# Issuing Silu and its product after the next pair's first eviction, and moving the norms' inverse roots to GpSimd, in the MLP of a hybrid decoder block

## The chip, the cores and the metric

One Trainium2 chip, 8 cores, one program on each core. A core takes one half of one of four sequences (4096 of 8192 positions, plus a halo). The metric is the device time of the slowest core in microseconds. Most executions agree within 0.3%. Some fall in a slower state, in which the cores of one die show a lower granted TensorE clock. They are marked slow in each list of runs and are not compared here. The engines are PE (matmul), PEld (its weight loads), DVE (VectorE), ACT (ScalarE), POOL (GpSimd) and SP (SyncE, which issues transfers).

## The reference, cut to what matters

The block has a convolution branch and an attention branch, an output projection, then a gated MLP with a causal depthwise convolution of width 3 between up projection and activation, then a last RMSNorm. The change touches only the MLP and the norms around it:

```python
h = rms_norm(x, norm_ffn_g[layer])
up = causal_dwconv(h @ w_up[layer], ffn_conv_w[layer], ffn_conv_b[layer])   # 1024 -> 2 x 2816
gate, val = jnp.split(up, 2, axis=-1)
x = x + (jax.nn.silu(gate) * val) @ w_down[layer]                            # 2816 -> 1024
...
return rms_norm(x, final_norm_g)
```

## The kernel before

The kernel runs in three stages: projections and attention; convolution branch, gates and output projection; MLP. The third takes 48% of the span. It goes over nine tiles of positions (388, then 3 x 384, then 5 x 512 columns). Each tile has 22 pairs of up projections (one gate channel block, one value channel block) and then the down projection. One pair, cut to the order of issue:

```python
def c_pair(j, p):
    for q in range(2):                       # 0: gate half, 1: value half
        b = next_ps()                        # one of 8 PSUM banks
        fm(ps[b], wU[wi], ...)               # PE: 8 matmuls
        t = next_tmp()                       # one of 5 temporaries
        ACT: uc[...] = last two columns of ps[b]              # for the next tile's corner
        ACT: tmpC[t] = w2 * ps[b] + bias                      # the eviction
        for sh, wv_ in ((1, w1_), (2, w0_)):
            DVE: tmpC[t] += wv_ * ps[b] shifted by sh         # the two taps
        POOL: tmpC[t][:, 0:2] += corr[:, ch, :]               # corner correction
        if q == 0:
            ACT: actT[:, p] = Silu(tmpC[t])
        else:
            POOL: actT[:, p] = actT[:, p] * tmpC[t]           # the product
```

In the traces ScalarE, VectorE and GpSimd run their instructions in the order in which the kernel issues them: in the pair that the prediction shows, the eviction of the value half (2333.27 us) starts only after Silu (2332.68 us), which had waited 2.93 us. The norm of a block is a Square with accumulation on ACT, an inverse root of six tiny operations on DVE (`rsq`), and a multiply on DVE. Blocks of the next tile are normed after pairs 12 and 16 and within the down projection. At the end of each output block of the down projection, Square, inverse root, multiply and the store follow at once, in one of 4 residual buffers:

```python
S.add("act", ... Square, accum_out=ssq[:, col:col + 1])
rsq(128, col)                                # six tiny operations on DVE
S.add("dve", ... xr[sl] = xr[sl] * rstd * g3b)
S.add("sp", ... dma_start(out=out_d[...], in_=xr[sl]))
xr_load()
```

The softmax here doesn't subtract the row's maximum and nothing guards it: scores larger than these inputs give would overflow.

Of the kernel before, what the change touches and what calls it, by code (L numbers as in the profile page):

```python
# [14 lines left out]
D = 1024  # L15
# [113 lines left out]
def build_program():  # L129
# [177 lines left out]

    RC = 0.703952253

    def rsq(n, col):  # L310
        v, y, t = ssq[0:n, col:col + 1], rstd[0:n, col:col + 1], rtmp[0:n, col:col + 1]
        vk, yk, tk = ("ssq", col), ("rstd", col), ("rtmp", col)
        S.add("dve", lambda e: e.tensor_scalar(out=v, in0=v, scalar1=D * EPS, scalar2=None, op0=ALU.add),
              reads=[vk], writes=[vk])
        S.add("dve", lambda e: e.tensor_scalar(out=y.bitcast(I32), in0=v.bitcast(I32), scalar1=-0.5,
                                               scalar2=float(0x5F1FFFF9), op0=ALU.mult, op1=ALU.add),
              reads=[vk], writes=[yk])
        for lim in (2.38924456, 3.0 / RC ** 2):
            S.add("dve", lambda e: e.tensor_scalar(out=t, in0=v, scalar1=y, scalar2=y, op0=ALU.mult, op1=ALU.mult),  # L319
                  reads=[vk, yk], writes=[tk])  # L320
            S.add("dve", lambda e: e.tensor_scalar(out=y, in0=t, scalar1=lim, scalar2=y, op0=ALU.subtract, op1=ALU.mult),  # L321
                  reads=[tk, yk], writes=[yk])

    def scale_g(gap, key):
# [70 lines left out]

    stat_i = [0]

    def norm_front(xap, xkey, hbap, hbkey, n, gb, gkey):
        col = stat_i[0] % 16
        stat_i[0] += 1  # L400
        S.add("act", lambda e: e.activation(out=hbap[0:n, :], in_=xap[0:n, :], func=AF.Square,  # L401
                                            accum_out=ssq[0:n, col:col + 1]),
              reads=[xkey], writes=[hbkey, ("ssq", col)])
        rsq(n, col)
        S.add("dve", lambda e: e.scalar_tensor_tensor(  # L405
            out=hbap[0:n, :], in0=xap[0:n, :], scalar=rstd[0:n, col:col + 1], in1=gb[0:n, :],
            op0=ALU.mult, op1=ALU.mult), reads=[xkey, ("rstd", col), gkey], writes=[hbkey])
        note("act", 1240)
        note("dve", 1450)

    def norm_back(hbap, hbkey, n, dst, dkeys):
        t = next_ps()
# [842 lines left out]
    hbC = [buf("hbC%d" % i, W + 39424 + i * 2048, [128, D], BF16) for i in range(2)]  # L1255
    g2b = buf("g2b", W + 43520, [128, D], F32)
    xn = [buf("xn%d" % i, W + 47616 + i * 4096, [128, D], F32) for i in range(2)]
    xr = [buf("xr%d" % i, W + 55808 + i * 4096, [128, D], F32) for i in range(4)]
    g3b = buf("g3b", W + 72192, [128, D], F32)
    tmpC.append(buf("tmpC4", W + 76288, [128, 512], F32))  # L1260
    sem_g2, sem_g3 = newsem("s_g2"), newsem("s_g3")
    sem_xn = [newsem("s_xn%d" % i) for i in range(2)]
    sem_xr = [newsem("s_xr%d" % i) for i in range(4)]
    sem_out = [newsem("s_out%d" % i) for i in range(4)]
    S.add("sp", lambda e: e.dma_start(out=g2b, in_=g2_d.partition_broadcast(128)), writes=[("g2b",)], dma_sem=sem_g2)
    scale_g(g2b, ("g2b",))
    tmp_set["n"] = 5
    xn_list = [(0, -1)] + [(j, b) for j in range(9) for b in BB[j]]
    xn_l, cf, cb = [0], [0], [0]

# [8 lines left out]
        S.add("sp", lambda e: e.dma_start(out=xn[sl][0:n, :], in_=x1_d[r0:r0 + n, :]), reads=[("x1_d", blk)],  # L1279
              writes=[("xn%d" % sl,)], dma_sem=sem_xn[sl])  # L1280

    def c_front():
        i = cf[0]
        cf[0] += 1
        j, blk = xn_list[i]
        n = 4 if blk < 0 else 128
        norm_front(xn[i % 2], ("xn%d" % (i % 2),), hbC[i % 2], ("hbC%d" % (i % 2),), n, g2b, ("g2b",))
        xn_load()

    def c_back():  # L1290
# [10 lines left out]
    def xr_load():  # L1301
        i = xr_l[0]
        if i >= len(xr_list):
            return
        xr_l[0] += 1
        j, blk = xr_list[i]
        sl = i % 4
        S.add("sp", lambda e: e.dma_start(out=xr[sl], in_=x1_d[4 + 128 * blk:132 + 128 * blk, :]),
              reads=[("x1_d", blk)], writes=[("xr%d" % sl, 0), ("xr%d" % sl, 1)], dma_sem=sem_xr[sl])

    fw = fcw.rearrange("p (c k) -> p c k", k=3)

    def c_pair(j, p):
        w_ = BW[j]
# [5 lines left out]
        for q in range(2):  # L1320
# [10 lines left out]
            S.add("act", lambda e, b=b, t=t, ch=ch, w2_=w2_: e.activation(  # L1331
                out=tmpC[t][:, 0:n], in_=ps[b][:, o:w_], func=AF.Identity, scale=w2_, bias=fcb[:, ch:ch + 1]),
                reads=[("ps", b), "fcw", "fcb"], writes=[tk])
            for sh, wv_ in ((1, w1_), (2, w0_)):
                lo = max(0, sh - o)
                S.add("dve", lambda e, b=b, t=t, sh=sh, wv_=wv_, lo=lo: e.scalar_tensor_tensor(  # L1336
                    out=tmpC[t][:, lo:n], in0=ps[b][:, o + lo - sh:w_ - sh], scalar=wv_, in1=tmpC[t][:, lo:n],
                    op0=ALU.mult, op1=ALU.add), reads=[("ps", b), tk, "fcw"], writes=[tk])
# [2 lines left out]
                                                                    in1=corr[:, ch, :], op=ALU.add),  # L1341
                      reads=["corr", tk], writes=[tk])
            res.append(t)
            if q == 0:
                S.add("act", lambda e, t=t: e.activation(out=actT[:, p, 0:n], in_=tmpC[t][:, 0:n], func=AF.Silu),  # L1345
                      reads=[tk], writes=[("actT", p)])
            else:
                S.add("pool", lambda e, t=t: e.tensor_tensor(out=actT[:, p, 0:n], in0=actT[:, p, 0:n],  # L1348
                                                             in1=tmpC[t][:, 0:n], op=ALU.mult),
                      reads=[tk, ("actT", p)], writes=[("actT", p)])  # L1350

    def c_corr(j):
        par = j % 2
# [18 lines left out]
    def c_down(j, hooks):  # L1372
        ub_ = 0
        for bi, blk in enumerate(BB[j]):
            i = xr_i[0]
            xr_i[0] += 1
            sl = i % 4
            banks = [next_ps(), next_ps()]
            parts = ([(0, 0, 20), (1, 0, 20), (0, 20, 22), (1, 20, 22)] if bi == 0 else [(0, 0, 22), (1, 0, 22)])
            for hf, ka, kb in parts:  # L1380
                for k_ in range(ka, kb):
                    wt, wk_, kk = wdn(k_)
                    S.add("pe", lambda e, b=banks[hf], k_=k_, kk=kk, wt=wt, hf=hf: e.matmul(  # L1383
                        ps[b], lhsT=actT[:, k_, bi * 128:(bi + 1) * 128], rhs=wt[:, kk, hf * 512:(hf + 1) * 512],
                        start=(k_ == 0), stop=(k_ == 21), skip_group_check=True),
                        reads=[wk_, ("actT", k_)], writes=[("ps", banks[hf])])
                if kb == 22:
                    xs_ = xr[sl][:, hf * 512:(hf + 1) * 512]
                    S.add("dve", lambda e, b=banks[hf], xs_=xs_: e.tensor_tensor(out=xs_, in0=ps[b], in1=xs_, op=ALU.add),
                          reads=[("ps", banks[hf]), ("xr%d" % sl, hf)], writes=[("xr%d" % sl, hf)])  # L1390
                    if hooks:
                        hooks.pop(0)()
            col = stat_i[0] % 16
            stat_i[0] += 1
            t = next_tmp()
            S.add("act", lambda e, sl=sl, t=t, col=col: e.activation(
                out=tmpC[t].bitcast(BF16), in_=xr[sl], func=AF.Square, accum_out=ssq[:, col:col + 1]),
                reads=[("xr%d" % sl, 0), ("xr%d" % sl, 1)], writes=[("tmpC%d" % t,), ("ssq", col)])
            rsq(128, col)
            S.add("dve", lambda e, sl=sl, col=col: e.scalar_tensor_tensor(  # L1400
                out=xr[sl], in0=xr[sl], scalar=rstd[:, col:col + 1], in1=g3b, op0=ALU.mult, op1=ALU.mult),
                reads=[("xr%d" % sl, 0), ("xr%d" % sl, 1), ("rstd", col), ("g3b",)],
                writes=[("xr%d" % sl, 0), ("xr%d" % sl, 1)])
            S.add("sp", lambda e, sl=sl, blk=blk: e.dma_start(out=out_d[128 * blk:128 * (blk + 1), :], in_=xr[sl]),
                  reads=[("xr%d" % sl, 0), ("xr%d" % sl, 1)], dma_sem=sem_out[sl])
            xr_load()
        for h_ in hooks:
            h_()

    xn_load()  # L1410
    xn_load()
    for _ in range(1 + len(BB[0])):
        c_front()
        c_back()
    S.add("sp", lambda e: e.dma_start(out=g3b, in_=g3_d.partition_broadcast(128)), writes=[("g3b",)], dma_sem=sem_g3)
    scale_g(g3b, ("g3b",))
    for _ in range(4):
        xr_load()
    for j in range(9):
        if j > 0:  # L1420
            c_corr(j)
        for p in range(22):
            c_pair(j, p)
            if j + 1 < 9 and p in (12, 16):
                c_front()
        hooks = []
        if j + 1 < 9:
            n = len(BB[j + 1])

            def mk(m):  # L1430
                def f():
                    if m < n:
                        c_back()
                        if m + 2 < n:
                            c_front()
                return f
            hooks = [mk(0), mk(1), (lambda: None), mk(2), (lambda: None), mk(3)][:(6 if n == 4 else 4)]
        c_down(j, hooks)
        assert cb[0] >= 1 + sum(len(BB[q]) for q in range(min(j + 2, 9))), (j, cb[0])

    final_wait = [(s_, S.dma_count[s_]) for s_ in sem_out if S.dma_count.get(s_, 0)]
# [164 lines left out]
```

## Time and profile before

| | before |
|---|---|
| median of 5 first runs | 2723.28 us (2721.09 to 2733.06) |
| MLP stage, first up projection to last matmul, slowest core | 1419.2 to 2713.4 us |
| PE busy in the span | 77% |
| one pair at 512 columns | 5.02 us, of which PE's work is 16 matmuls |

The chain that ended last, asked for in the MLP stage alone, by line (share of that stretch):

```profile
by line: DVE arena L1336 21.2%; PE ps L1383 17.5%; issue 16.1%; PE ps L602 13.3%; POOL arena L1348 9.7%; ACT arena L1331 8.2%; POOL arena L1340 4.5%; ACT uc L1329 2.8%; PE ps L414 1.2%; DMA arena<-g 1.0%; DVE rtmp L319 0.8%; ACTq L1503 0.7%
```

L1336 are the taps, L1331 the evictions, L1340 the corrections, L1348 the products, L602 and L1383 the up and down matmuls. The other lines on which the case rests stand in the prediction. One is missing there: its cut of a pair leaves out the eviction of the value half, which starts as Silu ends and on which the first two taps of the group at 2334.14 us work. (The eviction that it shows, 2333.98 us, is already that of the next pair's gate half.)

```profile
2333.27 0.77 ACT L1331 ACTIVATE arena<-ps,fcb_s,fcw_s 128x512 f32<-128x512 f32 x1
```

### The profile page before, as it was taken

Reading aid. Unit: us, or ns where it says so; the run is one execution under the profiler, and the core shown is the slowest. Engines: PE = TensorE matmul, PEld = TensorE weight load, DVE = VectorE, ACT = ScalarE, POOL = GpSimd, SP = SyncE. Lnnn points to the kernel's source line nnn. Section 1 sums busy time; section 2 is a strip of 40 time slices with the busy share of each in tenths; the row PEclk is TensorE's granted clock in tenths of the full one; section 3 lists DMA queues with packets and bytes.
Section 4 is the critical chain, followed back from the end, with each engine's and each line's share of the span. In section 5 each row is a group of like instructions: output and inputs, shape, how many; then the busy total and the mean of one; then the engine's idle time right before and its main releaser. Section 6 shows DMA issues by size and latency. Waiting matters only on the chain.

```text
span 2721.7 us, 37992 instructions; the slowest of 8 cores (2705.1 to 2721.7 us)
## 1 busy us (share of the span) xinstructions
PE 2099.5 (77%) x11389; PEld 1050.1 (39%) x11550; DVE 1358.3 (50%) x2561; ACT 843.9 (31%) x1791; POOL 483.3 (18%) x826
## 2 busy tenths in 40 slices
PE   0677787854799999999946868686968778697877
PEld 0344444432455544444423434343424333242433
DVE  4554555511444444443325555555655565555554
ACT  1343344413222221112214343334332433323232
POOL 1000002304221111111211121222121212212131
PEclk9988898976899999999979999999999999899999
DMA  8443473496362223310595101010102010020100
GB/s 144 120 112 86 106 160 66 98 161 130 102 129 78 87 86 102 102 51 34 108 174 112 63 9 62 16 55 16 63 16 78 8 54 33 16 78 16 62 1 31
DMA packets 128319, 205.88 MB, mean 76 GB/s; under 512 B 9684, under 2 KB 90330, under 8 KB 127736
## 3 DMA queue, kind: packets, MB, share of 16 engines
q1 hardware_dynamic: 86072, 169.19, 21.3%
q0 software_dynamic: 42048, 34.26, 9.3%
q8 instruction: 98, 1.61, 0.3%
q14 instruction: 101, 0.83, 0.1%
HBM read 177.05 MB, written 60.63 MB: 87 GB/s over the span
## 4 chain that ended last, share of the span: by engine, by line
PE 47%; DVE 18%; issue 12%; POOL 8%; ACT 7%; DMA 7%; DVEq 1%; SPq 1%; ACTq 0%; POOLq 0%
PE ps L602 29%; DVE arena L1336 10%; PE ps L1383 8%; POOL arena L1348 5%; ACT arena L1331 4%; PE ps L1198 3%; PE ps L608 3%; DMA u_d<-arena 2%; POOL arena L1340 2%; DMA arena<-h_d 2%; PE ps L414 2%; ACT uc L1329 1%; DVE rtmp L319 1%; DVE rstd L321 1%; DVE arena L405 1%
## 5 line engine op out<-in xcount | busy, mean ns | idle before, releaser
L602 PE MATMUL ps<-arena 128*128 128x512 bf16 (+5 forms) x6749 | 1388.0, 362 | 232.9 <-DVE arena L1336 202.1
L602 PEld LDWEIGHTS ps<-arena 128*128 128x128 bf16 x6848 | 657.9, 99 | 929.4 <-issue 327.7
L1336 DVE SCALAR_TENSOR_TENSOR arena<-ps,fcw_s,arena 128x511 f32<-128x511 f32 (+4 forms) x792 | 530.4, 688 | 412.0 <-ACT uc L1329 263.1
L1383 PE MATMUL ps<-arena 128*128 128x512 bf16 x1372 | 329.1, 395 | 68.0 <-POOL arena L1340 33.7
L1345 ACT ACTIVATE arena<-arena 128x512 bf16<-128x512 f32 (+1 forms) x198 | 115.2, 582 | 583.5 <-POOL arena L1340 533.7
L1331 ACT ACTIVATE arena<-ps,fcb_s,fcw_s 128x512 f32<-128x512 f32 (+1 forms) x396 | 279.9, 731 | 0.0
L1383 PEld LDWEIGHTS ps<-arena 128*128 128x128 bf16 x1408 | 141.2, 101 | 243.9 <-issue 98.1
L1348 POOL TENSOR_TENSOR arena<-arena 128x512 bf16<-128x512 bf16 (+1 forms) x198 | 208.8, 1054 | 138.3 <-DVE arena L1336 95.8
L1340 POOL TENSOR_TENSOR arena<-arena,corr 128x2 f32<-128x2 f32 x352 | 69.3, 197 | 856.6 <-DVE arena L1336 812.7
L1166 DVE TENSOR_TENSOR arena<-ps,arena 128x512 f32<-128x512 f32 (+2 forms) x144 | 91.0, 633 | 251.7 <-PE ps L602 245.6
L1152 ACT ACTIVATE arena<-ps,bg_s 128x512 f32<-128x512 f32 (+2 forms) x144 | 92.1, 640 | 252.4 <-PE ps L602 252.4
L414 PE MATMUL ps<-ident,arena 128*128 128x128 bf16 (+2 forms) x656 | 62.1, 250 | 140.2 <-DVE arena L405 135.1
L252 ACT ACTIVATE arena<-ps 128x512 bf16<-128x512 f32 (+4 forms) x152 | 82.7, 544 | 214.0 <-PE ps L602 126.1
L608 PE MATMUL ps<-arena 128*128 128x256 bf16 (+2 forms) x676 | 122.1, 336 | 34.1 <-DMA arena<-h_d 32.9
L485 ACT ACTIVATE arena<-ps 128x512 bf16<-128x512 f32 x192 | 109.8, 595 | 118.2 <-PE ps L482 60.1
L506 PE MATMUL ps<-arena 128*128 128x66 bf16 x768 | 60.2, 206 | 92.7 <-DVE arena L489 46.0
L1169 POOL TENSOR_TENSOR arena<-arena 128x512 bf16<-128x512 f32 (+2 forms) x72 | 82.7, 1149 | 263.9 <-DVE arena L1166 237.9
L401 ACT ACTIVATE arena<-arena 128x1024 bf16<-128x1024 f32 (+1 forms) x82 | 86.3, 1053 | 137.1 <-PE ps L414 117.4
L489 POOL TENSOR_TENSOR arena<-arena,mask 128x512 bf16<-128x512 bf16 x64 | 72.1, 1153 | 278.0 <-ACT arena L485 277.7
L1198 PE MATMUL ps<-arena 128*128 128x512 bf16 (+1 forms) x514 | 116.8, 379 | 3.3 <-POOL arena L1169 2.5
L254 DVE CAST arena<-ps 64x512 bf16<-64x512 f32 (+1 forms) x95 | 65.4, 688 | 104.4 <-PE ps L602 81.2
L414 PEld LDWEIGHTS ps<-ident,arena 128*128 128x128 bf16 (+2 forms) x656 | 51.2, 114 | 164.1 <-issue 156.4
(86 smaller groups left out, 1255.7 us busy)
## 6 DMA issues: line engine op xcount, KB each, us to landing
arena<-x_loc SPq DMA_DIRECT2D x80, 512.0 KB, 4.4
arena<-x_d SPq DMA_DIRECT2D x64, 512.0 KB, 3.6
x_d<-arena SPq DMA_DIRECT2D x32, 512.0 KB, 4.2
out<-arena SPq DMA_DIRECT2D x32, 512.0 KB, 2.6
u_d<-arena SPq DMA_DIRECT2D x96, 132.0 KB, 3.1
arena<-u_d SPq DMA_DIRECT2D x32, 396.0 KB, 3.4
arena<-w_up POOLq DMA_DIRECT2D x22, 512.0 KB, 18.1
arena<-w_in POOLq DMA_DIRECT2D x10, 1024.0 KB, 27.9
```

Of the source, the lines that this page charges most:

```text
L414: S.add("pe", lambda e, kc=kc: e.transpose(out=psb[t][:, kc * 128:kc * 128 + n], in_=hbap[0:n, kc * 128:(kc + 1) * 128], identity=ident[0: ...
L485: S.add("act", lambda e: e.activation(out=PA[pi], in_=ps[sbk], func=AF.Exp, scale=0.125), reads=[("ps", sbk)], writes=[("PA%d" % pi,)])
L602: S.add("pe", lambda e, kc=kc: e.matmul(out, lhsT=wap[:, kc, col0:col0 + 128], rhs=rhs(kc), start=(kc == 0), stop=(kc == kcn - 1), skip_gr ...
L608: S.add("pe", lambda e, kc=kc: e.matmul(out, lhsT=lhs(kc), rhs=wap[:, kc, c0:c0 + n], start=(kc == 0), stop=(kc == KC - 1), skip_group_che ...
L1152: S.add("act", lambda e, b=b, t=t, br=br: e.activation(out=tmp[t][:, 0:w_], in_=ps[b][:, 0:w_], func=AF.Sigmoid, bias=bg[:, br * 8 + oc:br ...
L1198: S.add("pe", lambda e, b=b, kc=kc, hf=hf: e.matmul(ps[b][0:n, :], lhsT=mT[:, kc, c0:c0 + n], rhs=wO[:, kc, hf * 512:(hf + 1) * 512], star ...
L1331: S.add("act", lambda e, b=b, t=t, ch=ch, w2_=w2_: e.activation(out=tmpC[t][:, 0:n], in_=ps[b][:, o:w_], func=AF.Identity, scale=w2_, bias ...
L1336: S.add("dve", lambda e, b=b, t=t, sh=sh, wv_=wv_, lo=lo: e.scalar_tensor_tensor(out=tmpC[t][:, lo:n], in0=ps[b][:, o + lo - sh:w_ - sh], ...
L1340: S.add("pool", lambda e, t=t, ch=ch: e.tensor_tensor(out=tmpC[t][:, 0:2], in0=tmpC[t][:, 0:2], in1=corr[:, ch, :], op=ALU.add), reads=["c ...
L1345: S.add("act", lambda e, t=t: e.activation(out=actT[:, p, 0:n], in_=tmpC[t][:, 0:n], func=AF.Silu), reads=[tk], writes=[("actT", p)])
L1348: S.add("pool", lambda e, t=t: e.tensor_tensor(out=actT[:, p, 0:n], in0=actT[:, p, 0:n], in1=tmpC[t][:, 0:n], op=ALU.mult), reads=[tk, ("a ...
L1383: S.add("pe", lambda e, b=banks[hf], k_=k_, kk=kk, wt=wt, hf=hf: e.matmul(ps[b], lhsT=actT[:, k_, bi * 128:(bi + 1) * 128], rhs=wt[:, kk, ...
```

## The change

Its intent is to keep PE fed in the MLP stage, by not letting Silu stand in front of an eviction that DVE waits for, and by taking small work and waits off DVE. The core of the diff (cut):

```diff
-    tmpC.append(buf("tmpC4", ...))            # 5 temporaries, 4 residual buffers
+    tmpC += [... for i in range(3)]           # 7 temporaries, 3 residual buffers
@@ c_pair
             ACT eviction of half q
+            if q == 0:
+                flush(late)                   # Silu and product of the pair before
             DVE taps, POOL correction
-            if q == 0: ACT Silu
-            else:      POOL product
+        def gate(): ACT Silu; POOL product
+        late.append(gate)
+        if p == 0:
+            flush(finals)
@@ norms of the next tile's blocks
-            if p in (12, 16): c_front()       # Square, root on DVE, multiply
+            if p in (11, 15): c_stat()        # Square, root on POOL
+            if p in (13, 17): c_mul()         # multiply on DVE
@@ c_down, per output block
     DVE add to the residual
+    flush(finals)
     ...
-    rsq(128, col); multiply; store; xr_load() # root on DVE
+    norm_stat(..., "pool", ...)               # root on POOL
+    finals.append(fin)                        # multiply, store, load: behind the next add
```

Inside the down projection the norms of the next tile's third and fourth block are split into statistics and multiply in the same way. Nothing else changes.

## The prediction

> **What bounds the kernel now.** I read the page's slices first, then the waits from 1425 us on, then the order of time inside one pair, and last stretches of time side by side.
>
> ```profile
> PE 2099.5 (77%) x11389; PEld 1050.1 (39%) x11550; DVE 1358.3 (50%) x2561; ACT 843.9 (31%) x1791; POOL 483.3 (18%) x826
> PE   0677787854799999999946868686968778697877
> PEclk9988898976899999999979999999999999899999
> ```
>
> The changed lines run only in the last stage, the gated MLP: from 1419.2 us (first up projection) to the end, 48% of the span. Slices of 9 for PE in the stage before give way to a saw of 6 to 8. Each tooth is one of nine token tiles (388, 3 x 384, 5 x 512 columns): the low part is 22 pairs of up projections, the high part is the down projection.
>
> ```profile
> ACT arena L1345 <- POOL arena L1340: 533.7, 176, 5.4
> DVE arena L1336 <- ACT uc L1329: 263.1, 148, 2.9
> PE ps L602 <- DVE arena L1336: 202.1, 133, 3.1
> PE ps L1383 <- POOL arena L1340: 33.7, 10, 4.6
> PE ps L1383 <- POOL arena L1348: 31.9, 14, 3.7
> ```
>
> In the waits, every engine waits for another: Silu (L1345) for the corrected gate half, VectorE's taps for ScalarE, PE for VectorE to empty PSUM. None is full. Such a ring is a latency loop; one pair shows it.
>
> ```profile
> 2332.39 0.20 POOL L1340 TENSOR_TENSOR arena<-arena,corr 128x2 f32<-128x2 f32 x1
> 2332.68 0.63 ACT L1345 ACTIVATE arena<-arena 128x512 bf16<-128x512 f32 x1 [2.93 <-POOL arena L1340]
> ...
> 2333.98 0.79 ACT L1331 ACTIVATE arena<-ps,fcb_s,fcw_s 128x512 f32<-128x512 f32 x1
> 2334.14 3.11 DVE L1336 SCALAR_TENSOR_TENSOR arena<-ps,fcw_s,arena 128x511 f32<-128x511 f32 x4 [1.91 <-ACT uc L1329]
> 2335.89 0.20 POOL L1340 TENSOR_TENSOR arena<-arena,corr 128x2 f32<-128x2 f32 x1 [3.30 <-DVE arena L1336]
> 2336.29 1.16 POOL L1348 TENSOR_TENSOR arena<-arena 128x512 bf16<-128x512 bf16 x1 [0.20 <-POOL arena L1340]
> 2337.41 0.20 POOL L1340 TENSOR_TENSOR arena<-arena,corr 128x2 f32<-128x2 f32 x1
> ```
>
> The loop: the corner correction of a gate half (2332.39) releases Silu; in-order ScalarE evicts the value half only after Silu; VectorE needs two taps; GpSimd corrects, multiplies, and only then (2337.41) corrects the next pair's gate half. Period 5.02 us. In it VectorE works 3.11, GpSimd about 1.6, ScalarE 0.63 + 4 short and long evictions, about 2 us, and PE 16 matmuls. PE, eight banks ahead, is held to this pace.
>
> ```profile
> 2409.00:2523.00 114.00, 86.19 (x363) 35.72 (x369) 67.66 (x104) 45.76 (x108) 30.15 (x60) 0.95 0.07 22
> 2410.26 10.74 PE ps L602 x49
> ```
>
> The first row is 114 us of a 512-column up stage (columns: stretch, then PE, PEld, VectorE, ScalarE, GpSimd busy, clock): PE busy 86, but with bursts and half-speed spells. The second, from the chain, is a free run: 10.74 / 49 = 0.2192 us for a 512-column matmul, so a pair could cost 3.51 us.
>
> **What the Trainium skill says.** "TensorE: Matmul & The Clock Gate", section "What's actually happening", says the matmul clock falls to half after an idle window of about 3.4 us. The trace agrees: 0.95 or 0.96 in up stages with gaps, 1.00 where PE is dense. Its section "Seeing it yourself" warns that three cores of a die with dense matmuls are limited to 13/16. This trace disagrees:
>
> ```profile
> 800.00:1300.00 500.00, 482.84 (x2490) 240.15 (x2526) 213.22 (x372) 103.12 (x158) 69.03 (x81) 1.00 0.28 81
> ```
>
> This is the slowest core in the stage before, at 97% PE; all eight cores show 482 to 485 us busy and clock 1.00 there. "SBUF — State Buffer", section "Who interferes with whom", says a VectorE instruction with two SBUF inputs blocks against a GpSimd one that reads SBUF. The taps have one PSUM input, and they stay at 752 ns at most beside GpSimd's products: agrees. The norm multiply has two SBUF inputs, and its 1.28 us could meet a 1.16 us product, up to about a microsecond each time. "GPSIMD Engine Reference", section "2.1 Instruction dispatch", describes software dispatch for each instruction; here a 128x2 correction lasts 197 ns, and dependent GpSimd operations start 0.40 us apart.
>
> **The change part by part.**
>
> 1. Silu and product of a pair are issued late: after the next pair's gate eviction. ScalarE no longer meets a correction that has just begun to be computed, and GpSimd's product no longer stands between a tap and Silu. The shortest remaining ring is product, correction, Silu, each once per pair: 1.16 + 0.20 + 0.63 + about 0.4 of hand-overs = 2.4 us. The ring through value eviction and taps now spans two pairs: about 5.1 / 2 = 2.6 us. Both lie under 3.51, so at 512 columns PE sets the pace. Two more temporaries (seven, as one residual buffer goes) cover the later release.
>
> 2. The 6-step inverse root moves from VectorE to GpSimd: the four lines cost VectorE 33.3 + 26.1 + 9.4 + 9.1 = 78 us in the stage, mostly in down stages where VectorE is slack, but 2 x 2 us in each up stage. On GpSimd I estimate 6 x 0.42 = 2.5 us, twice in an up stage. It holds up the next correction: some 1.3 us of hole for VectorE each.
>
> 3. Norm statistics and multiply are split by two pairs, and the final multiply waits for the next addition. So VectorE no longer stands waiting 4 to 5 us at a tile's start, where it finishes the last block before pair 0 (2409.0 to 2414.2). One 1.28 us multiply goes behind pair 0.
>
> 4. Residual slots 4 to 3: a block takes 44 x 0.2192 = 9.65 us, a slot has two blocks, 19 us, for a store of 2.6 and a load of 3.6. Hidden.
>
> **Tile times.** Tile starts, read from PE's chain, are 1419.2, 1549.4, 1679.1, 1808.5, 1938.8, 2094.5, 2252.0, 2408.9, 2566.1, and the last matmul ends at 2713.4.
>
> 512 columns: up 352 x 0.2192 = 77.2; down 176 x 0.2192 = 38.6; four transposes of blocks at about 0.45 extra (2388.87 to 2389.31) = 1.8. Sum 117.6, taken as 118, four times, against 155.7 to 157.5. VectorE has 22 x 3.11 + 3 x 1.28 = 72.3, under 77.2. Down starts with 40 matmuls, 8.8 us, before it needs the last two pairs, which are ready about 4 us after the last up matmul. So its wait (65.6 us in all, the last two wait lines) goes too. Last tile, no transposes: 116 against 147.3.
>
> 384 columns: a free run is 17.06 us for 104 (164 ns), so 352 x 0.164 = 57.7, down 132 x 0.2192 = 28.9, transposes 1.4: 88.0. VectorE is level here: four taps in 2.58, a pair at about 2.61, PE's pair 2.62. With 3 x 1.28 of multiplies and 2 x 1.3 of holes VectorE needs 64 us, starts 2.2 us behind PE, and PE's down would need the last pairs at 66.5; I add a wait of about 1.5. Three tiles at 89.5, 89.5 and 91 (the last has a transpose right before the next tile), against 129.8, 129.4, 130.3.
>
> Tile 0: its first eviction stays at 1431.4, as ScalarE waits there for a DMA of g. Then VectorE, 22 x 2.61 + 5, to about 1495, and the rest of down 21 + 1.4: end near 1518, 98.5 us against 130.2. The down weights land by about 1465, before they are needed.
>
> Sum: 98.5 + 270 + 472 + 116 = 956.5 against 1294.2: 337.7 saved. The tail after the last matmul (8.3 us) grows by 0.6, as the inverse root takes 2.5 instead of 1.93 on it. 2723.3 - 337.7 + 0.6 = 2386. I add 4 us for hand-overs I don't see: 2390.
>
> **The rivals.** (a) The clock: if the denser last stage trips the 13/16 limit, its matmuls take 1.23 times as long: 950 x 0.23 = 218 us back, about 2610. Against it stands the 500 us stretch at 1.00 on all cores; for it, that VectorE and ScalarE are busier in this stage. (b) VectorE or GpSimd becomes the bound: if small GpSimd operations with a register operand last a microsecond, an inverse root blocks the corrections 6 us, twice a tile, and VectorE, level at 384, cannot catch up: 4 to 6 us a tile, about 2430. The 0.2 us rows speak against. (c) The wait only moves: products come later, so PE waits before down as now. That would give back up to 65.6 us, about 2455; but that wait came from VectorE lagging four pairs, which a PE-bound loop does not build up. (d) Nothing gained since PE is bound: excluded by 3.51 against 5.02.
>
> **Range and chances.** The sum is bounded by PE from below: no tile can beat it, except by my additions, so low is 2372. Above, (b) and part of (c) give 2430. Only (a) in full leaves that range, and even it is 4% faster. Predicted 2390, range 2372 to 2430; faster 0.97, same 0.02, slower 0.01.
>
> **What would show it.** PE's slices from 1430 us should read 9, the clock 1.00, a 512 tile 118 us, a 384 tile about 90, the span of a pair 3.5. ScalarE's wait for the correction and PE's for VectorE should nearly vanish, the latter staying in 384 tiles if anywhere. Inverse-root steps appear on GpSimd at 0.2 to 0.3 us. If pairs still take over 4 us, I missed a ring; if PE's matmuls are slower than 0.22 us in free runs, it is the clock.

## More of the kernel before

No line dominates: the chain walks around all four engines. That is what a latency ring looks like in this view.

## The result, and the profile after

| | before | after |
|---|---|---|
| median of all runs | 2727.38 us (16 runs, 5 of them slow) | 2370.15 us (9 runs, 2 of them slow) |
| profiled run | 2723.27 us | 2365.35 us |
| ratio of fast runs | | 0.8688, 95% interval 0.8674 to 0.8703 |
| MLP stage, slowest core | 1294.2 us | 938.1 us |

A ratio is the mean time of one kernel's fast runs over that of the other's in the same rounds, so it is not quite the ratio of the medians. The change is 13.1% faster; the two slow runs of the changed kernel took 2529.08 and 2700.80 us, the five of the kernel before 2773.41 to 2921.54. The prediction said 2390, with 2372 as its low end: the result lies 2 us below the range.

The page of the changed kernel: busy time, then PE's and the clock's slices. The MLP stage begins at the end of slice 24 of 40, the 3 among the nines.

```profile
PE 2040.4 (86%) x11550; PEld 1050.1 (44%) x11550; DVE 1275.0 (54%) x2195; ACT 856.2 (36%) x1791; POOL 613.8 (26%) x1192
PE   0578768794659999999999939999999999999998
PEclk9999889997759999999999969999999999999999
```

The saw is gone: PE reads 9 from the entry of the stage on, but for the last slice (8), which holds the tail. The chain of the MLP stage is now PE alone for long pieces (columns: start, length, what):

```profile
by line: PE ps L608 55.1%; PE ps L1409 29.8%; issue 3.2%; DVE arena L1358 3.0%; PE ps L420 1.4%; DMA arena<-g 1.3%; DVE arena L409 0.9%; DMA arena<-x_d 0.9%; POOL arena L1371 0.8%; ACT arena L1351 0.6%; POOL arena L1362 0.3%; POOL rtmp L319
...
1893.26 75.97 PE ps L608 x352
```

A whole up stage of 352 matmuls at 512 columns (L608) is one piece of 75.97 us with no wait in it. The waits of the stage, which answer to the list in the prediction (L1362 correction, L1369 Silu, L1358 taps, L1371 product):

```profile
ACT arena L1369 <- POOL arena L1362: 95.7, 82, 3.3
...
DVE arena L1358 <- ACT uc L1349: 30.6, 14, 13.3
...
PE ps L1409 <- POOL arena L1362: 2.8, 3, 0.9
...
PE ps L608 <- DVE arena L1358: 1.5, 1, 1.5
...
PE ps L1409 <- POOL arena L1371: 0.6, 1, 0.6
```

Silu's wait fell from 533.7 to 95.7 us, the taps' from 263.1 to 30.6, PE's for the taps from 202.1 to 1.5, and PE's before the down projection from 65.6 (33.7 + 31.9) to 3.4. What is left of Silu's wait costs nothing: ScalarE has work to spare. In order of time, two Silus of a 512 tile (columns: start, length, engine, line):

```profile
1962.84 0.63 ACT L1369 ACTIVATE arena<-arena 128x512 bf16<-128x512 f32 x1 [1.29 <-POOL arena L1362]
...
1965.57 0.63 ACT L1369 ACTIVATE arena<-arena 128x512 bf16<-128x512 f32 x1 [0.58 <-POOL arena L1362]
```

Just after a norm multiply has held up DVE, the engines catch up at 2.73 us a pair (1962.84 to 1965.57), against PE's 3.45 (75.97 / 22). Such room is what keeps the ring off PE. The busy time of the stretches (columns: stretch, length, PE, PEld, DVE, ACT, POOL busy with counts, granted clock, DMA share, GB/s), a 384 tile and a 512 tile:

```profile
1598.00:1687.00 89.00, 87.67 (x511) 48.58 (x509) 63.63 (x103) 45.61 (x122) 42.69 (x106) 1.00 0.16 54
...
1893.00:2009.00 116.00, 116.00 (x563) 53.51 (x561) 81.64 (x108) 57.53 (x126) 51.45 (x118) 1.00 0.16 55
```

PE fills the 512 tile entirely, and the clock reads 1.00. Tile by tile, from the first up matmul of one tile to that of the next, slowest core of each profile:

| tile (columns) | before | predicted | after |
|---|---|---|---|
| 0 (388) | 130.2 | 98.5 | 93.3 |
| 1 to 3 (384) | 129.8, 129.4, 130.3 | 89.5, 89.5, 91 | 88.6, 88.9, 90.2 |
| 4 to 7 (512) | 155.7, 157.5, 156.9, 157.2 | 118 each | 115.7, 115.8, 115.7, 115.8 |
| 8 (512, no norms) | 147.3 | 116 | 114.1 |

### The profile page after: what moved, and what is told of

The parts are those of the page before. It is cut to its first block, busy times and chain, and to the rows that moved or that the text cites. A ratio compares the mean times of both kernels' runs of the same rounds, so it can differ in the third digit from the quotient of the medians.

```text
span 2363.8 us, 38182 instructions; the slowest of 8 cores (2345.9 to 2363.8 us)
## 1 busy us (share of the span) xinstructions
PE 2040.4 (86%) x11550; PEld 1050.1 (44%) x11550; DVE 1275.0 (54%) x2195; ACT 856.2 (36%) x1791; POOL 613.8 (26%) x1192
## 4 chain that ended last, share of the span: by engine, by line
PE 73%; DVE 9%; issue 7%; DMA 6%; ACT 2%; POOL 2%; SPq 1%; DVEq 1%; ACTq 0%; POOLq 0%
PE ps L608 50%; PE ps L1409 12%; PE ps L1204 4%; PE ps L614 4%; DMA arena<-h_d 2%; PE ps L420 2%; DMA u_d<-arena 1%; DVE arena L1358 1%; DVE arena L409 1%; POOL arena L495 1%; DMA arena<-g 1%; DVE rtmp L319 1%; PE ps L488 1%; PE ps L512 1%; DVE rstd L321 1%
## 5 line engine op out<-in xcount | busy, mean ns | idle before, releaser
L608 PE MATMUL ps<-arena 128*128 128x512 bf16 (+5 forms) x6848 | 1349.5, 358 | 3.7 <-DVE arena L424 2.0
L608 PEld LDWEIGHTS ps<-arena 128*128 128x128 bf16 x6848 | 664.2, 98 | 654.6 <-issue 17.1
L1358 DVE SCALAR_TENSOR_TENSOR arena<-ps,fcw_s,arena 128x511 f32<-128x511 f32 (+4 forms) x792 | 524.8, 687 | 108.1 <-ACT uc L1349 30.6
L1409 PE MATMUL ps<-arena 128*128 128x512 bf16 x1408 | 311.3, 379 | 4.0 <-POOL arena L1362 2.8
L401 ACT ACTIVATE arena<-arena 128x1024 bf16<-128x1024 f32 (+1 forms) x114 | 119.9, 1052 | 342.3 <-DVE arena L1415 205.2
L1371 POOL TENSOR_TENSOR arena<-arena 128x512 bf16<-128x512 bf16 (+1 forms) x198 | 210.3, 1062 | 109.4 <-ACT uc L1349 73.2
L1369 ACT ACTIVATE arena<-arena 128x512 bf16<-128x512 f32 (+1 forms) x198 | 115.2, 582 | 112.7 <-POOL arena L1362 95.7
L1362 POOL TENSOR_TENSOR arena<-arena,corr 128x2 f32<-128x2 f32 x352 | 84.4, 243 | 202.0 <-DVE arena L1358 190.1
```

The source lines that it names most:

```text
L401: S.add("act", lambda e: e.activation(out=junk[0:n, :], in_=xap[0:n, :], func=AF.Square, accum_out=ssq[0:n, col:col + 1]), reads=[xkey] + ...
L608: S.add("pe", lambda e, kc=kc: e.matmul(out, lhsT=wap[:, kc, col0:col0 + 128], rhs=rhs(kc), start=(kc == 0), stop=(kc == kcn - 1), skip_gr ...
L1358: S.add("dve", lambda e, b=b, t=t, sh=sh, wv_=wv_, lo=lo: e.scalar_tensor_tensor(out=tmpC[t][:, lo:n], in0=ps[b][:, o + lo - sh:w_ - sh], ...
L1369: S.add("act", lambda e: e.activation(out=actT[:, p, 0:n], in_=tmpC[tg][:, 0:n], func=AF.Silu), reads=[("tmpC%d" % tg,)], writes=[("actT", ...
L1371: S.add("pool", lambda e: e.tensor_tensor(out=actT[:, p, 0:n], in0=actT[:, p, 0:n], in1=tmpC[tv][:, 0:n], op=ALU.mult), reads=[("tmpC%d" % ...
L1409: S.add("pe", lambda e, b=banks[hf], k_=k_, kk=kk, wt=wt, hf=hf: e.matmul(ps[b], lhsT=actT[:, k_, bi * 128:(bi + 1) * 128], rhs=wt[:, kk, ...
```

## The experiments

The first theory is that of the prediction: the ring over Silu, value eviction, taps and correction was the bound; the late issue breaks it; PE takes over. Rivals: the norms' move to GpSimd and their split carry a good part; GpSimd's product in front of the next correction was the real holder; VectorE, not PE, is the bound now. Times of all runs, fast runs only for the ratios:

| run | median us | ratio to before, 95% interval |
|---|---|---|
| after_again (the changed kernel) | 2363.65 | 0.8688 (0.8665 to 0.8711) |
| late_only | 2367.07 | 0.8695 (0.8669 to 0.8722) |
| root_dve | 2368.21, 4 runs, one of them slow | 0.8695 (0.8664 to 0.8727) |
| half_late | 2423.80, 5 runs, one slow | 0.8904 (0.8880 to 0.8928) |
| no_late | 2729.09 | 0.9986 (0.9926 to 1.0045) |
| product_late | fast runs 2710.07, 2721.97 | none given, two of four slow |
| product_late_2 | fast runs 2711.99, 2704.38 | none given, three of five slow |
| one_tap (wrong results) | 2358.56, 3 runs, one slow | 0.8614 (0.8534 to 0.8694) |
| seven_k (wrong results) | 2331.32, 3 runs, one slow | 0.8522 (0.8444 to 0.8600) |
| after_third (the changed kernel) | 2361.78, 5 runs, one slow | 0.8671 (0.8643 to 0.8699) |
| early_entry | 2338.55 | 0.8596 (0.8566 to 0.8625) |

In the rounds of no_late, product_late, one_tap and seven_k, three of the seven runs of before (2738 to 2752 us) counted as fast but show one die's clock at 0.90 to 0.92. Against the mean of the other four (2724.1 us) the means of the fast runs come to 1.002, 0.997, 0.864 and 0.855. No reading below changes by that.

### The changed kernel as reference

> The changed kernel itself, as the reference on this chip for the other runs: 2362 to 2373 in fast runs, ratio about 0.869.

> The changed kernel again, as the reference for the run beside it: 2361 to 2373 in fast runs.

The medians, 2363.65 and 2361.78 us, came as expected; single fast runs lie below, down to 2356.23. Tile times in after_again (slowest core): 93.2, 88.6, 88.9, 90.2, four of 115.7 to 115.8, 114.1.

### late_only: one part of the change alone

```diff
 # the kernel before
             ACT eviction of half q
+            if q == 0:
+                flush(late)
             ...
-            if q == 0: ACT Silu
-            else:      POOL product
+        late.append(gate)          # Silu and product of this pair
```

> The kernel before with one part of the change: Silu and product of a pair are issued after the next pair's gate eviction; inverse root on VectorE, five temporaries, four residual slots, everything else as before. Theory (the ring of Silu, value eviction, taps and correction was the bound, and breaking it is nearly the whole gain): PE-bound in the 512-column tiles, 115.7 to 117 us each as in the changed kernel; the 384-column tiles some 2 to 6 us longer than the changed kernel's 88.6 to 90.2, as VectorE still does the inverse roots. Time 2370 to 2395, ratio to before 0.870 to 0.880. Rival (the move to GpSimd and the split of the norms carry an important share, a third or more): 2480 or more.

Measured 2367.07 us, ratio 0.8695 beside 0.8688 of the full change on the same chip: the intervals overlap almost wholly. That is just under the expected 2370 to 2395. The late issue is the whole gain, with 5 temporaries and all roots on VectorE. The tiles show where the rest of the change does a little: 95.8, 89.8, 89.4, 90.7 in the first four (sum 365.7, against 360.9 in after_again), and 115.7 to 115.8 in the 512 tiles, not different at all. These are the slowest cores of two profiles, 4.8 us apart; the timed runs don't resolve it.

### no_late: the whole change without that part

```diff
 # the changed kernel
-            if q == 0:
-                flush(late)
+            if q == 0: ACT Silu
+            else:      POOL product
-        late.append(gate)
```

> The changed kernel without the late Silu and product: each is issued in its own half of the pair as before; roots on GpSimd, split norms, late final multiply, seven temporaries stay. Theory (the ring is the bound): pairs again 5.0 us at 512 columns and 4.3 at 384; the ring starts 2 to 3 us earlier in each tile since VectorE does not stand at the tile's start, while two roots on GpSimd lengthen the ring by 2 to 3 us each: 2690 to 2730, ratio 0.985 to 1.003. Rival (temporaries and norm placement carry a third of the gain): 2610 or less.

Measured 2729.09 us, within the expected 2690 to 2730, ratio 0.9986, interval across 1. Two more temporaries, roots on GpSimd, split norms and late finals give nothing while the ring binds. Its 512 tiles take 155.8 to 159.3 us, much as before; tile 0 is 4 us shorter (126.5), its 384 tiles are 1 to 4 us longer (131.0, 131.3, 134.6). In order of time the root on GpSimd then lies on the ring (product, first and last step of the root, correction, Silu):

```profile
2319.87 1.17 POOL L1368 TENSOR_TENSOR arena<-arena 128x512 bf16<-128x512 bf16 x1 [0.20 <-POOL arena L1360]
2321.00 0.23 POOL L313 TENSOR_SCALAR ssq<-ssq 128x1 f32<-128x1 f32 x1
...
2323.27 0.29 POOL L321 TENSOR_SCALAR rstd<-rtmp,rstd 128x1 f32<-128x1 f32 x1 [0.17 <-POOL rtmp L319]
2323.64 0.20 POOL L1360 TENSOR_TENSOR arena<-arena,corr 128x2 f32<-128x2 f32 x1
2323.92 0.63 ACT L1365 ACTIVATE arena<-arena 128x512 bf16<-128x512 f32 x1 [4.53 <-POOL arena L1360]
```

The correction that releases Silu comes 2.6 us later than the product's end would have let it, and Silu waits 4.53 us in place of 2.93. So the two runs together take the gain apart: all of it is in the order of Silu and the product.

### root_dve: the inverse root back on VectorE

```diff
-    def c_stat(eng="pool"):
+    def c_stat(eng="dve"):
-            col = norm_stat(xr[sl], ..., 128, "pool", ...)
+            col = norm_stat(xr[sl], ..., 128, "dve", ...)
```

> The changed kernel with the inverse root back on VectorE in this stage. Theory: VectorE has slack at 512 columns (about 66 us of taps in 76 us), so those tiles stay at 115.7; at 384 columns, where taps take 54.6 of 57.4 us, 4 + 2 x 2 us more on VectorE lengthen the tiles by 2 to 6 us each: total 2 to 24 us above the changed kernel, 2372 to 2394. Rival (the roots on GpSimd hold up the corrections and cost more than they give): equal to the changed kernel or faster, with less VectorE idle before taps in the 384 tiles.

Measured 2368.21 us, ratio 0.8695 against 0.8688. The direction of the tiles is the theory's (tile 0: 96.1 in place of 93.2; 384 tiles 89.2, 89.0, 91.4 in place of 88.6, 88.9, 90.2; 512 tiles unchanged), but it is 0.1 to 3 us a tile, and the timed difference is within the noise. The time lies under the 2372 to 2394 that I expected; in the timed runs the rival's "equal" came true, though not its "faster". For the time, the move of the root is neutral.

### product_late: only GpSimd's product is delayed

```diff
 # the kernel before; Silu stays where it is
             POOL correction
+            if q == 0:
+                flush(late)                   # the product of the pair before
-            else:      POOL product
+            else:      late.append(prod)
```

> The kernel before with only GpSimd's product delayed behind the next pair's gate correction, Silu staying in front of the value eviction. Theory: the product ends only some 0.1 to 0.2 us after VectorE's taps of the next gate half, so taking it out of the ring uncovers the taps: period 5.0 to 4.85-4.9 us, total 15 to 40 us less, 2685 to 2712. Rival (GpSimd's order, the product ahead of the correction, is what holds the ring): period 5.02 - 1.16 - 0.2 = about 3.7 us, PE nearly bound, total 2440 or less.

> The same kernel as in the earlier run with only the product delayed, whose timed runs had fallen in the slow state: in fast runs, as its profile showed (period 5.00 us against 5.02, tiles 0.5 to 2.5 us shorter), 2703 to 2715; rival as before, 2440 or less.

Fast runs of the two: 2710.07, 2721.97, 2711.99, 2704.38. Means of the fast runs against the means of before in the same rounds: 2716.0 / 2733.6 = 0.994 and 2708.2 / 2721.3 = 0.995. The rival's 2440 is excluded; the second forecast (2703 to 2715) holds. The first profile shows why, in order of time:

```profile
2323.58 0.19 POOL L1346 TENSOR_TENSOR arena<-arena,corr 128x2 f32<-128x2 f32 x1 [1.31 <-DVE arena L1342]
2323.74 1.16 POOL L1357 TENSOR_TENSOR arena<-arena 128x512 bf16<-128x512 bf16 x1
2323.87 0.63 ACT L1353 ACTIVATE arena<-arena 128x512 bf16<-128x512 f32 x1 [2.91 <-POOL arena L1346]
...
2328.87 0.63 ACT L1353 ACTIVATE arena<-arena 128x512 bf16<-128x512 f32 x1 [2.92 <-POOL arena L1346]
```

The product now lies behind the correction, and the correction waits for DVE's taps instead. The period is 5.00 us (2323.87 to 2328.87) in place of 5.02. Two releasers of nearly equal lateness stood in front of the correction, and taking the later one away uncovered the other. I had expected 4.85 to 4.9, from a distance of 0.1 to 0.2 us between the two; the second stood even closer, since the correction starts 0.14 us after the taps end.

### half_late: Silu right behind the value eviction of its own pair

```diff
 # the changed kernel
-            if q == 0:
-                flush(late)
-        late.append(gate)
+        gate()                                # after both evictions of this pair
```

> The changed kernel, but Silu and product of a pair are issued right after the value eviction of the same pair, half a pair earlier. Theory: the order to break is Silu ahead of the value eviction; what is left is a ring Silu, next gate eviction, taps, correction of about 0.54 + 0.72 + 0.15 + 1.55 + 0.4 = 3.4 us at 512 columns, just under PE's 3.45, and about 2.95 us at 384, over PE's 2.61. So 512 tiles unchanged, 384 tiles 3 to 8 us longer: 2375 to 2400. Rival (a full pair of delay is needed; half of it leaves most of the wait): 2450 or more.

Measured 2423.80 us, ratio 0.8904: 60 us above the changed kernel, and above my range of 2375 to 2400. The rival's 2450 is not reached either. The ring is as computed. Silu to Silu in order of time, four lines at 384 columns and then two at 512:

```profile
1563.19 0.52 ACT L1367 ACTIVATE arena<-arena 128x384 bf16<-128x384 f32 x1 [1.25 <-POOL arena L1360]
...
1563.92 1.27 DVE L409 SCALAR_TENSOR_TENSOR arena<-arena,rstd 128x1024 bf16<-128x1024 f32 x1
...
1566.87 0.52 ACT L1367 ACTIVATE arena<-arena 128x384 bf16<-128x384 f32 x1 [1.91 <-POOL arena L1360]
...
1569.88 0.52 ACT L1367 ACTIVATE arena<-arena 128x384 bf16<-128x384 f32 x1 [1.25 <-POOL arena L1360]
...
1964.33 0.63 ACT L1367 ACTIVATE arena<-arena 128x512 bf16<-128x512 f32 x1 [1.41 <-POOL arena L1360]
...
1967.83 0.63 ACT L1367 ACTIVATE arena<-arena 128x512 bf16<-128x512 f32 x1 [1.41 <-POOL arena L1360]
```

3.01 us at 384 (expected 2.95; PE needs 57.36 / 22 = 2.61) and 3.50 at 512 (expected 3.4; PE needs 3.45). My sum went wrong in a plain way: I counted the ring's excess over PE and nothing else. This ring has no slack, so what interrupts it adds to the time as well. The first period shown has one norm multiply of 1.27 us in it and takes 3.68 us, 0.67 longer than the next. A tile has two such multiplies, a late final, two Squares and two roots on its pairs. So tile 0 takes 99.3 us, the 384 tiles 100.2 to 102.4 and the 512 tiles with norms 118.9 to 121.0, which sums to the 60 us. The ring's own excess, 22 x (3.01 - 2.61) = 8.8 us, is most of the loss of a 384 tile (11.3 to 12.2). The rest I put down to the interruptions, not each of them measured; that the last tile, without norms, takes 114.1 us as in the changed kernel speaks for it. Half a pair later gives five sixths of the gain; a full step, with slack in the ring, is needed for the rest.

### one_tap and seven_k: who binds now

```diff
 # one_tap
-            for sh, wv_ in ((1, w1_), (2, w0_)):
+            for sh, wv_ in ((1, w1_),):
 # seven_k
-               [("wU%d" % wi, q)] + h2k, b=b)
+               [("wU%d" % wi, q)] + h2k, kcn=7, b=b)
```

> The changed kernel without the second VectorE tap (wrong results on purpose), so half of the taps' work is gone. Theory (PE is the bound of the stage now): 512 tiles unchanged at 115.7, the wait of about 0.9 us before the down projection of 384 tiles goes, tile 0 some 3 us less: 3 to 10 us less than the changed kernel, 2355 to 2368. Rival (VectorE is the bound or a co-bound): 40 us less or more.

> The changed kernel with 7 of the 8 matmuls of each up projection (wrong results on purpose): PE's up work falls from 76.0 to 66.5 us at 512 and from 57.4 to 50.2 at 384, VectorE's stays. Theory: PE is the bound with VectorE close behind: 512 tiles gain 6 to 9.5 us each (taps and multiplies need some 70 us, down hides the rest), 384 tiles and tile 0 gain little, 0 to 3 us, since VectorE's 54.6 + 4 us then bind: total 30 to 55 us less, 2310 to 2338. Rival (PE alone binds, VectorE is far off): 76 us less, about 2290.

Taking away half of the taps, over 260 us of DVE work (a half of 524.8), leaves the 512 tiles at 115.7 to 115.8 us. Only tile 0 (89.7 in place of 93.2) and the 384 tiles (87.0, 87.0, 88.7) are shorter, 8.5 us in all; fast runs 2349.55 and 2358.56. Taking away one in eight up matmuls gives some 34 us by the sum of the tiles (fast runs 2326.38 and 2331.32). Its tiles: 93.4, 90.2, 89.0, 90.2, then 108.4, 109.4, 109.4, 109.4, and 104.6 in the last, which has no norms. So PE binds the 512 tiles: the last tile gives back the whole of 9.5 us. With norms in a tile, DVE comes into sight after 6.4 of them. At 384 columns PE and DVE bind together: neither cut gives much, and seven_k's first such tile is even 1.6 us longer. The waits of seven_k show it, PE waiting for the taps again:

```profile
PE ps L608 <- DVE arena L1358: 16.3, 11, 3.8
...
PE ps L1409 <- POOL arena L1362: 7.6, 6, 1.7
```

### early_entry: a version that beats both

In the changed kernel the longest idle time of PE in this part lies at the entry of the stage, from 1378.5 to 1416.4 us. PE waits there for four normed blocks, and ScalarE for the load of the gain, while the weights of the MLP come in as well:

```profile
PE ps L420 <- DVE arena L409: 33.6, 4, 17.9
ACT arena L325 <- DMA arena<-g: 31.8, 1, 31.8
```

The edit moves the entry under the end of the stage before. The inputs of these blocks were written to DRAM in the first tile of that stage.

```diff
 # the changed kernel
+    during the last tile's gates: load g2b and the first blocks, scale g2b, norm two blocks
+    within the last output projection: transposes, norm of the other two blocks
-    after it: g2b, loads, four times (statistics, multiply, transposes)
-    scale_g(g3b, ("g3b",))                    # at once: ScalarE waits for its load
+            if j == 0 and p == 10:
+                scale_g(g3b, ("g3b",))
```

> A version meant to beat both: the changed kernel, with the entry of the last stage moved under the end of the stage before (gain vector, first norm blocks and their transposes run during the last gates and the last output projection) and the scaling of the final gain moved from the start of tile 0 to its middle. In the changed kernel PE stands some 37 us between the last output projection (1378.5) and the first up projection (1416.4). Theory: the gap goes, but the down weights, which land near 1465, then hold PE for some 10 to 20 us before the first down projection: net 12 to 25 us less, 2340 to 2355. Rival (the gap is set by the weight transfers alone): equal within 5 us.

Measured 2338.55 us, ratio 0.8596 beside 0.8671 for the changed kernel on the same chip and rounds. That is 0.9% less (0.8596 / 0.8671 = 0.991; the intervals do not touch), 20 us in the means of the fast runs (2359.6 and 2339.1), and correct. The first up projection now starts at 1378.0 us. The size was as expected (12 to 25 us less), but by luck, for a wrong reason. I had expected the down weights to hold PE. They don't; the new wait is another:

```profile
ACT arena L1365 <- POOL arena L1385: 13.2, 1, 13.2
...
PE ps L608 <- DVE arena L1372: 8.8, 1, 8.8
```

GpSimd stands at the issue of the last weight transfers until 1404.7 us and works its products (L1385) off only then. The temporaries run out, ScalarE stops for 13.2 us, and PE for 8.8. That wait is still to be had.

## Why the prediction was right or wrong

**The bound and the mechanism: right.** A latency ring held the MLP stage, the late issue of Silu and product broke it, and PE took over (late_only 0.8695, no_late 0.9986; a 512 up stage is one piece of 75.97 us). Waits vanished as written. One link of the loop was read too simply: the prediction had the next correction come after GpSimd's product ("only then (2337.41)"). By product_late, DVE's taps stand there 0.02 us behind, so that to take the product out of the way, by itself, is worth 0.02 us a pair at 512 columns; what counts is that Silu no longer stands before the value eviction.

**Where it failed: the matmul's time.** The failed step is "The second, from the chain, is a free run: 10.74 / 49 = 0.2192 us for a 512-column matmul, so a pair could cost 3.51 us." The changed kernel shows 75.97 / 352 = 0.2158 between starts. The hardware did not get faster: in the trace of before the matmuls of that piece start 0.2158 us apart too. What I divided was not 49 steps. The length of a piece runs to the end of its last matmul, and that end is modelled, 379 ns after its start (the median below). So 49 matmuls make 48 steps and one such length: (10.74 - 0.379) / 48 = 0.2158. The next piece of the chain, which the prediction does not show, begins 10.79 us after the first:

```profile
2421.05 10.74 PE ps L602 x49
```

10.79 / 0.2158 is 50: one record is missing between the two pieces, and that is why they end there. Such gaps are common in this trace. It has 1408 weight loads of the down projection but 1372 matmuls, and the reference's shapes ask for 32 x 44 = 1408:

```profile
L1383 PEld LDWEIGHTS ps<-arena x1408: 95/98/152, 1513.1 to 2712.7; 128*128 128x128 bf16 x176
L1383 PE MATMUL ps<-arena x1372: 376/379/634, 1513.5 to 2713.0; 128*128 128x512 bf16 x196
```

But the missing records are not the error. The same down block in the two traces, in order of time, before and then after:

```profile
2389.31 9.66 PE L1383 MATMUL ps<-arena 128*128 128x512 bf16 x43
```

```profile
2230.84 9.66 PE L1409 MATMUL ps<-arena 128*128 128x512 bf16 x44
```

It takes 9.66 us in both, and the complete one of 44 also divides to a wrong 0.2195, while (9.66 - 0.379) / 43 = 0.2158. My "a block takes 44 x 0.2192 = 9.65 us" would have looked like a confirmation; both have the same end in them. The piece of 352 escapes this: it begins at the modelled end of the matmul before it (its own first start is 1893.10), so that its length is 352 steps. Everything I called "bounded by PE from below" was too high by 1.6%: 1760 up and 1408 down matmuls at 512 columns times 0.0034 us are 10.8 us. That alone would have put the forecast at 2379, and the low end, drawn from the same floor, at 2361, under the measured 2370. "Perfetto Trace Analysis", section "Identifying the Most-Contended Engine", says that matmul busy time is not a good measure of how close a kernel is to its peak, because matmuls are pipelined. This agrees: a matmul is shown 379 ns long, and the next one starts 216 ns after it.

**VectorE at 384 columns: off by 5%.** "Four taps in 2.58, a pair at about 2.61" has the same fault: 2.58 us is a group of four with its last tap counted to the end. In an unbroken run the chain of after shows two taps every 1.24 us (1612.75, 1613.97, 1615.22, ...), so a pair takes 2.49. Over 22 pairs this is 2.6 us, half of what tile 0 was off (predicted 98.5, measured 93.3). The extra waits in the 384 tiles came, somewhat smaller: PE stood about 0.9 us before the down projection, predicted 1.5.

**The addition for "hand-overs I don't see": not there.** The 4 us have no counterpart. Together: the stage came out 938.1 in place of 956.5 us (tile 0 5.2 less, 384 tiles 2.3, 512 tiles 9.0, last tile 1.9), and the 4 us go. The stage began at 1416.4 on this core against 1419.2 on that of before, which is no effect of the change. From 2390, minus 18.4, 4 and 2.8, plus 0.4 for the tail, is 2365.2; the profiled run had 2365.35.

**Parts 2 and 3: the times right, the worth overrated.** The root on GpSimd was put at 2.5 us; from 1937.68 to 1940.22 it takes 2.54 us:

```profile
1937.68 0.22 POOL L313 TENSOR_SCALAR ssq<-ssq 128x1 f32<-128x1 f32 x1
...
1939.93 0.29 POOL L321 TENSOR_SCALAR rstd<-rtmp,rstd 128x1 f32<-128x1 f32 x1 [0.17 <-POOL rtmp L319]
```

It puts a hole into DVE's work as written, but DVE has room for it. The tail after the last matmul grew by 1.0 us (8.3 to 9.3), predicted 0.6. All that these parts do for the time is 0 to 5 us in the first four tiles. That DVE "no longer stands waiting 4 to 5 us at a tile's start" is true and off the path. The prediction said that the norm multiply could meet GpSimd's product, "up to about a microsecond each time". In the changed kernel it does meet GpSimd: each of the 32 operations that GpSimd starts during a norm multiply in this stage takes 0.7 to 1.0 us longer (a correction 1.10 us in place of 0.20, a product 1.77 in place of 0.92), 28 us in all:

```profile
1551.61 1.27 DVE L409 SCALAR_TENSOR_TENSOR arena<-arena,rstd 128x1024 bf16<-128x1024 f32 x1
...
1551.83 1.10 POOL L1362 TENSOR_TENSOR arena<-arena,corr 128x2 f32<-128x2 f32 x1 [0.99 <-DVE arena L1358]
```

In the kernel before no GpSimd operation of the stage overlaps such a multiply. In late_only none is lengthened, and its time is the same within the noise, so the 28 us lie off the path.

**Part 4 and the rivals.** Three residual slots cost nothing that the runs show (late_only has four, and the same time). The clock (a) stayed at 1.00 in the dense stage. That the trace agrees with the idle window of 3.4 us is more than the prediction's 0.95 and 1.00 show: in the trace of before, matmul starts go from 0.216 to 0.427 us apart 1 us after a wait of 2.75 us (ended at 2327.38), and stay at 0.216 behind one of 2.74 us (ended at 2350.91). Gaps cost clock here; which length of gap does, these traces don't settle. GpSimd (b) and the moved wait (c) did not come: their 4 to 6 us a tile and up to 65.6 us were 0.9 us a 384 tile. The range was drawn too narrowly downward: I took PE's floor for certain to 1%, with the reading behind it unchecked.

## What to carry to other kernels

When every engine waits for another and none is full, write down the ring of one iteration with its start times, and look for the instruction that stands in order in front of work it does not feed; moving it one step later was worth 13% here, and the rest of the change nothing measurable. Before a releaser in front of a wait is taken away, look for the second-latest: it may be 0.02 us behind. Take a rate from start to start: a short piece's length holds the full end of its last instruction, here 1.6% of a floor that was called certain. And hold the number of records against the number that the program issues.

## What the Trainium skill lacked or had wrong

- "TensorE: Matmul & The Clock Gate", section "Back-to-back issue gap", gives about 131 ns for each 512-column matmul as a measured sustained rate in a stream of weight loads and matmuls. Here such a stream takes 75.97 / 352 = 215.8 ns; the page's other figure, 215.7 ns, holds.
- The same page, section "Seeing it yourself", tells to budget 13/16 of the clock for dense matmuls on all cores. With all eight cores dense, the stretches of the fast runs read 1.00 for 500 us (PE 482 to 485 us busy), and in the changed kernel for 844 us more (1510 to 2354 us, PE 822 to 840 us busy on the eight cores). Whether one die's mean clock at 0.80 to 0.81 in a run of 2700.8 us is this limit, no run here shows.
- "Perfetto Trace Analysis" warns that matmul spans are modelled, not that matmul records can be missing while the weight loads are complete: 1372 and 1408 in the down projection of before, 11389 and 11550 in the whole program. Nor does it say what that model does to a rate: 49 matmuls in 10.74 us read as 219 ns each, at 216 ns between starts.
- "GPSIMD Engine Reference" has no measured time of a whole tiny operation. Here a 128x1 operation with a per-partition operand lasts 294 or 341 ns (medians of two kinds) on GpSimd and 214 or 273 on VectorE, and the dependent chain of six takes 2.54 us against 1.93.
- "SBUF — State Buffer", section "Who interferes with whom": that taps with one PSUM input do not meet GpSimd's products holds here too (at most 752 ns before and after, with GpSimd busier). That a multiply with two SBUF inputs does meet them holds as well, and the page has no size for it: here a correction that starts during the multiply takes 1.10 us in place of 0.20 (32 such operations, 0.7 to 1.0 us each), while those that started before it keep their length.
